# A hybrid attention layer: the mixing stage by a list schedule, its first merge moved forward, and two thresholds by bit search on ScalarE

## The chip, the core and the metric

The kernel runs on one core of a Trainium2 chip. The metric is the device time of one execution in microseconds (us); a time is the median of three runs. The engines are named as in the profile: PE multiplies matrices, PEld loads its weights, DVE is VectorE, ACT is ScalarE, POOL is GpSimd, SP issues DMAs. Each has its own queue of instructions.

## The reference, cut to what matters

One layer on 1024 tokens, ahead of which 16 meta tokens stand (1040 positions), with 1024 channels. Two half-step feed-forward parts (FFN1, FFN2; 2816 wide) stand around a mixing part:

```python
h = h + 0.5 * swiglu(rmsnorm(h, norm_ffn1[l]), ...)
u = rmsnorm(h, norm_mix[l])
qa, ka, va, qi, ki, wi, qs, ksw, vsw, ga, gb = jnp.split(u @ w_in[l], IN_SPLITS, axis=-1)
...                                     # rope on all queries and keys
o_sparse = sparse_branch(qa, ka, va, qi, ki, wi, pos, kvalid, topk)    # topk = 256
o_swa = swa_branch(qs, ksw, vsw, sinks[l], pos, kvalid)                # window 128, with sinks
merged = sigmoid(ga) * (o_sparse @ w_branch_sparse[l]) + sigmoid(gb) * (o_swa @ w_branch_swa[l])
h = h + merged @ w_out[l]
h = h + 0.5 * swiglu(rmsnorm(h, norm_ffn2[l]), ...)
```

The sparse branch works on blocks of 128 queries. An index score, the sum over 4 heads of relu(qi ki) wi, is computed for each query and key; each query keeps the 256 keys of the highest score (ties go to the lower position), and attention of 8 heads is taken over these.

## The kernel before

Positions lie along the free dimension, in two halves of 528 (with the meta tokens) and 512. Every f32 operand of a product is kept as a pair of f16 tiles, high and low part, and a product is three matmuls (`mm3`, L145 to L147). A weight is loaded by SP into `wst`; `split_w` (L130, L131) makes the pair `wsp`: ACT copies the high part, DVE computes the low one. `wsp` has four buffers, `wst` two.

The stages are FFN1, the mixing stage and FFN2. In the two FFN stages the kernel fixes the order of the engines' instructions by hand (`tc.manual_schedule(engines=ORDERED)`: PE, DVE, ACT, POOL). In the mixing stage it does not: the framework's scheduler orders what `layer_kernel` writes down, within the limits of the buffers. FFN1 ends with its down projection, the matmuls `pdn`; DVE adds each to `h`, and the squares of `h` are summed into `acc`. From that `norm_stats` makes `n_r` (a sum over the partitions on PE, `nsum`; small operations; a broadcast by PE, `nbc`) and `norm_u` the normed `un` and its pair `u`.

The mixing stage then consists of these pieces:

- `k_half`, `q_half`: projections (`rp`), rope (`rt` on DVE and POOL, `ry` on ACT) and a way through DRAM (`qscr`, `kscr`) that lays heads and rows out for the scores. `pv_t` is the value projection.
- `score(b)` for block b = 1 to 7 of the sparse branch: PE computes `ps_i`, ACT the ReLU `rel`, DVE sums into `sc`, 128 queries by 16 + 128 (b + 1) keys.
- `swa_block(b)`: scores `ps_s`, DVE adds mask and finds the maximum (`psw`), ACT exponentiates and sums (`a_sm`), PE transposes (`ptr`), ACT and DVE make the pair (`pts`), PE multiplies by the values, and the result is transposed into `oT` (`otr`).
- Thresholds. Block 0 needs none. Blocks 1 to 4 use `by_max`: rounds of MAX8 (the 8 largest of each row) and MATCH_REPLACE8 (strike them out), on DVE alone. Blocks 1 and 2 drop the lowest; block 3 (528 keys) and block 4 (656 keys) take 32 rounds each. Blocks 5 to 7 use `search((5, 6, 7))`: the 32 bits of each row's 256th largest score are found one after another. For each bit ACT runs a Sign pass over each block's scores with a sum (`jk`, L812), DVE compares the sum and makes the next candidate with operations of three columns (`s5d`, `s5key`, `s5nb`). `select(b, kth)` then turns scores into a mask (0 or a large negative number), ties included.
- `sparse_block(b)`: like `swa_block`, with `ps_a`, the mask added by DVE (`psp`, `b_mx`), `b_sm`, `ptb`.
- `swa_merge(d)` for 8 groups of channels: a gate (`p_gate`, tanh into `gt`), the branch's projection (`p_br`), their product `mg`. The same for the sparse branch, then the sum of both as a pair `mt`, and `p_out`, the projection back, added to `h`.

In `layer_kernel`'s text the first half's merge of the sparse branch (8 times 36 matmuls of 512 columns) and its projection (8 times 24) stand behind sparse block 7, in the same loop over the halves as the second half's.

Of the kernel before, what the change touches and what calls it, by code (L numbers as in the profile page):

```python
# [16 lines left out]
P = 128  # L17
# [14 lines left out]

WS = 256.0
# [6 lines left out]
F_GROUPS = ((0, 6), (6, 12), (12, 18), (18, 22))  # L40

# [14 lines left out]
def layer_kernel(ctx: ExitStack, tc: tile.TileContext, xT, gains, wgu1, wd1, win, wvi, wbs, wbw, wout,  # L56
                 wgu2, wd2, sinks, rope, m_swa0, m_swa, m_sp0, eye, out):
    nc = tc.nc
# [3 lines left out]
    ph = {}  # L62

# [22 lines left out]
    def mcst(shape, dt, name, bufs=1):
        return ph["sb"].tile(shape, dt, tag=name, name=name, bufs=bufs)

    def mmps(name):
        return ph["ps"].tile([P, 512], F32, tag="mm", name=name, bufs=3)  # L90

    def qkps(name):
        return ph["ps"].tile([P, 512], F32, tag="qk", name=name, bufs=2)

    def trps(name):
        if not ph["mix"]:
            return ph["ps"].tile([P, ph["S"], 512], F32, tag="w", name=name, bufs=8 // ph["S"])[:, 0, :]
# [19 lines left out]
    ident = cst.tile([P, P], F32, name="ident")  # L117
    nc.sync.dma_start(ident, eye)
    g_all = cst.tile([P, 4, KD], F32, name="g_all")
    nc.sync.dma_start(g_all, gains)  # L120
    ones = cst.tile([P, 1], F32, name="ones")
    nc.vector.memset(ones, 1.0)

    def load_raw(src, n):
        st = big.tile([P, 1024], F32, tag="wst", name="wst", bufs=2)
# [8 lines left out]
    def wsp_tile():  # L134
        return big.tile([P, 2, 1024], F16, tag="wsp", name="wsp", bufs=4)
# [27 lines left out]
    def new_acc():  # L163
        return big.tile([P, 528], F32, tag="acc", name="acc", bufs=2)
# [31 lines left out]
    def fpage(shape, dt, name):  # L196
        return ph["sb"].tile(shape, dt, tag="fp", name=name, bufs=27)

    def ftmp(name):
        return ph["sb"].tile([P, 528], F32, tag="ft", name=name, bufs=6)  # L200

    def fbtmp(name):
        return ph["sb"].tile([P, 528], F32, tag="fb", name=name, bufs=5)

    def wide(name):
        return ph["ps"].tile([P, ph["S"], 512], F32, tag="w", name=name, bufs=8 // ph["S"])
# [20 lines left out]
    def ffn(u, rb, hs, gi, wgu, wd, other_half, passes, saved):  # L227
# [10 lines left out]
        def new_hid(x):  # L238
# [6 lines left out]
            return big.tile(shape, F16, tag="nt", name="hid", bufs=2)  # L245
# [101 lines left out]
        def sum_tiles():  # L347
            return [ph["sb"].tile([P, 1024], F32, tag="wS", name=n_, bufs=2) for n_ in ("sa", "sb")]

        def late_tiles():  # L350
            return (ph["sb"].tile([P, 2, 1024], F16, tag="ws", name="x3", bufs=2),
                    ph["sb"].tile([P, 2, 512], F16, tag="w4", name="x4", bufs=2))
# [268 lines left out]
    hsp = dram.tile([KD, P, T], F32, name="hspill")  # L621
# [9 lines left out]
    open_phase("mix")  # L631

# [36 lines left out]
    def stack_q(ys, qt):  # L669
        scr = dram.tile([2, 2, P, 512], F16, tag="qscr", name="qscr", bufs=3)  # L670
# [6 lines left out]
    def stack_k(ys, kts, w):  # L677
        scr = dram.tile([2, P, 2, w], F16, tag=f"kscr{w}", name="kscr")
# [84 lines left out]
    def score(b):  # L763
        w = META + P * (b + 1)
        raw = ph["sb"].tile([P, w], F32, tag=f"sc{b}", name=f"sc{b}")
# [30 lines left out]
    def search(bs):  # L796
# [53 lines left out]
    def select(b, kth):  # L850
        w = META + P * (b + 1)
        raw = sc[b][0]
        gt = ph["sb"].tile([P, T], F16, tag="jk", name="gt", bufs=1)[:, :w]
        eq = ph["sb"].tile([P, T], F16, tag="eq", name="eq", bufs=1)[:, :w]
# [39 lines left out]
    def pttile(name):  # L894
        return ph["sb"].tile([P, 2, 1024], F16, tag="PT", name=name, bufs=2)

    def swa_block(b, qs, oT):
# [28 lines left out]
        pv = ph["ps"].tile([P, 512], F32, tag="pv", name="pv_s", bufs=1)  # L926
# [27 lines left out]
    def sparse_block(b, qa, oT):  # L954
# [6 lines left out]
        pv = ph["ps"].tile([P, 512], F32, tag="pv", name="pv_b", bufs=1)  # L961
# [25 lines left out]
    def new_oT():  # L987
        return ph["sb"].tile([P, 2, 4, 512], F16, tag="oT", name="oT", bufs=3)
# [14 lines left out]
    oT_w = []  # L1003
    for x in range(2):
# [16 lines left out]
    kth = search((5, 6, 7))  # L1021
    merged = [[], []]

    def swa_merge(d):
        gw, bw = load_w(win[12 + d], 1024), load_w(wbw[d], 512)
        for x in range(2):
            mg = hp([P, 512], F32, "mg")
# [4 lines left out]
    by_max(1)  # L1032
    by_max(2)
    sparse_block(0, qa, oT_s[0])
    sparse_block(1, qa, oT_s[0])
    sparse_block(2, qa, oT_s[0])
    swa_merge(0)
    swa_merge(1)
    swa_merge(2)
    by_max(3)  # L1040
    sparse_block(3, qa, oT_s[0])
    swa_merge(3)
    by_max(4)
# [158 lines left out]
```

## Time and profile before

| | us |
|---|---|
| median of 3 runs | 2033.18 (2031.63 to 2033.3) |
| profiled execution | 2033.16 |
| its span, first to last instruction | 2031.1 |
| PE busy | 1936.5 (95%) |
| DVE busy | 1627.2 (80%) |
| ACT busy | 901.0 (44%) |
| POOL busy | 386.9 (19%) |
| mixing stage, 682 to 1382: DVE busy | 574.8 |
| mixing stage, 682 to 1382: ACT busy | 422.4 |

Times in the trace count from the first instruction. The busy time of PE is that of matmuls that overlap, so it is no measure of how closely they follow each other. The mean clock granted to PE is 0.99 of full speed in the mixing stage.

### The profile page before, as it was taken

How to read it: one execution, taken by the hardware profiler on the slowest of the kernel's cores; microseconds unless marked ns; L12 is line 12 of the kernel's file. 1: busy time of each engine (PE TensorE's matmuls, PEld its weight loads, DVE VectorE, ACT ScalarE, POOL GpSimd, SP SyncE). 2: the span in 40 equal slices, each digit the busy share in tenths (PEclk: the TensorE clock that was granted, in tenths of full speed). 3: DMA queues.
4: the chain of work that ended last, by engine and by line, in shares of the span. 5: the costliest groups of instructions: out<-in, count | busy, mean ns of one | idle time of the engine just before them, and what ended most of it. 6: DMA issues, size and time to landing. Idle time of an engine off the chain costs nothing.

```text
span 2031.1 us, 32839 instructions
## 1 busy us (share of the span) xinstructions
PE 1936.5 (95%) x13080; PEld 1197.3 (59%) x13080; DVE 1627.2 (80%) x2779; ACT 901.0 (44%) x1602; POOL 386.9 (19%) x313
## 2 busy tenths in 40 slices
PE   5899999999999989899999999998899999999997
PEld 4588888888888556454545654444344444444443
DVE  7888788778875799999999964566987787788767
ACT  4433233333323446589885643433433243233232
POOL 3611312221310132221001000002322212312200
PEclk9999999999999999999999999999999999999998
DMA  4011111111113543212020024241112121111213
GB/s 158 11 63 48 58 63 50 55 64 58 48 63 105 183 141 112 99 59 73 17 63 17 27 68 156 78 164 49 34 55 68 48 72 47 63 62 47 76 38 130
DMA packets 58873, 146.95 MB, mean 72 GB/s; under 512 B 7264, under 2 KB 13408, under 8 KB 58720
## 3 DMA queue, kind: packets, MB, share of 16 engines
q1 hardware_dynamic: 58720, 144.86, 22.3%
q8 instruction: 102, 1.67, 0.3%
q14 instruction: 51, 0.42, 0.1%
HBM read 130.01 MB, written 14.76 MB: 71 GB/s over the span
## 4 chain that ended last, share of the span: by engine, by line
PE 70%; DVE 18%; ACT 4%; issue 4%; DMA 2%; POOL 2%; DVEq 0%; SPq 0%; ACTq 0%; POOLq 0%
PE pc L327 14%; PE pd L327 14%; PE pa L327 14%; PE pb L327 7%; PE p_br L999 2%; DVE sc L791 2%; DVE u L222 2%; DVE wsp L131 1%; PE p_gate L147 1%; PE p_gate L145 1%; PE p_gate L146 1%; DVE m L790 1%; PE p_out L146 1%; PE p_out L147 1%; PE p_out L145 1%
## 5 line engine op out<-in xcount | busy, mean ns | idle before, releaser
L327 PEld LDWEIGHTS <-wsp 128*128 128x128 f16 x4176 | 410.0, 98 | 214.2 <-issue 12.3
L327 PEld LDWEIGHTS <-x 128*128 128x128 f16 x3132 | 307.3, 98 | 157.9 <-issue 8.5
L327 PE MATMUL pa<-u,wsp 128*128 128x264 f16 (+1 forms) x1440 | 224.7, 310 | 0.0
L131 DVE SCALAR_TENSOR_TENSOR wsp<-wst,wsp 128x1024 f16<-128x1024 f32 (+2 forms) x130 | 134.8, 1038 | 54.6 <-ACT wsp L130 54.3
L130 ACT ACTIVATE wsp<-wst 128x1024 f16<-128x1024 f32 (+2 forms) x130 | 111.7, 863 | 140.1 <-PE p_out L147 45.9
L147 PEld LDWEIGHTS <-wsp 128*128 128x128 f16 x912 | 90.5, 99 | 94.5 <-issue 12.3
L145 PEld LDWEIGHTS <-wsp 128*128 128x128 f16 x912 | 91.0, 100 | 85.1 <-issue 4.1
L146 PEld LDWEIGHTS <-wsp 128*128 128x128 f16 x912 | 90.7, 99 | 80.2 <-issue 3.9
L327 PE MATMUL pb<-tb,wsp 128*128 128x264 f16 (+1 forms) x720 | 113.7, 312 | 8.1 <-ACT tb L235 5.5
L327 PE MATMUL pc<-tb,x 128*128 128x264 f16 (+1 forms) x720 | 113.9, 313 | 6.6 <-DVE c L458 6.4
L327 PE MATMUL pc<-tb,wsp 128*128 128x256 f16 (+1 forms) x720 | 114.2, 314 | 0.0
L327 PE MATMUL pd<-tb,x 128*128 128x256 f16 (+1 forms) x720 | 110.7, 308 | 0.0
L327 PE MATMUL pd<-u,x 128*128 128x256 f16 (+1 forms) x720 | 110.7, 308 | 0.0
L289 POOL TENSOR_TENSOR t<-g,g 128x512 f32<-128x512 f32 x16 | 25.5, 1595 | 436.0 <-DVE g L494 436.0
L812 ACT ACTIVATE jk<-sc,s5nb 128x784 f16<-128x784 f32 (+2 forms) x93 | 97.9, 1052 | 19.0 <-DVE s5nb L827 15.3
L341 ACT ACTIVATE wsp<-sa 128x1024 f16<-128x1024 f32 (+1 forms) x62 | 60.2, 971 | 103.4 <-DVE sa L393 103.4
L327 PE MATMUL pa<-hid,wsp 128*128 128x264 f16 (+1 forms) x648 | 103.1, 310 | 0.0
L341 ACT ACTIVATE wsp<-wst 128x1024 f16<-128x1024 f32 (+1 forms) x62 | 59.9, 967 | 94.3 <-DMA wst<-in_wgu_dram 49.9
L327 PE MATMUL pd<-hid,x 128*128 128x256 f16 (+1 forms) x648 | 101.6, 308 | 0.0
L147 PE MATMUL p_gate<-u,wsp 128*128 128x512 f16 x256 | 97.0, 379 | 1.4 <-DVE wsp L131 1.4
L145 PE MATMUL p_gate<-u,wsp 128*128 128x512 f16 x256 | 97.0, 379 | 0.0
L146 PE MATMUL p_gate<-u,wsp 128*128 128x512 f16 x256 | 97.0, 379 | 0.0
(234 smaller groups left out, 4147.6 us busy)
## 6 DMA issues: line engine op xcount, KB each, us to landing
wst<-in_wgu_dram SPq DMA_DIRECT2D x88, 512.0 KB, 3.7
wst<-in_win_dram SPq DMA_DIRECT2D x44, 512.0 KB, 3.5
wst<-in_wd_dram SPq DMA_DIRECT2D x48, 384.0 KB, 3.4
wst<-in_wd_dram SPq DMA_DIRECT2D x32, 256.0 KB, 2.7
wst<-in_wout_dram SPq DMA_DIRECT2D x16, 512.0 KB, 4.1
qscr<-ry SPq DMA_DIRECT2D x20, 256.0 KB, 2.1
q<-qscr SPq DMA_DIRECT2D x20, 256.0 KB, 3.0
wst<-in_wbs_dram SPq DMA_DIRECT2D x16, 256.0 KB, 2.7
```

Of the source, the lines that this page charges most:

```text
L130: nc.scalar.activation(sp[:, 0, :n], st[:, :n], AF.Copy, scale=WS)
L131: nc.vector.scalar_tensor_tensor(sp[:, 1, :n], st[:, :n], WS, sp[:, 0, :n], op0=ALU.mult, op1=ALU.subtract)
L145: nc.tensor.matmul(ps, w[:, 0, wcols], xt[:, 0, xcols], start=start, stop=False)
L146: nc.tensor.matmul(ps, w[:, 0, wcols], xt[:, 1, xcols], start=False, stop=False)
L147: nc.tensor.matmul(ps, w[:, 1, wcols], xt[:, 0, xcols], start=False, stop=stop)
L222: nc.vector.tensor_sub(u[k][:, 1, s0:s1], t[:, :w], u[k][:, 0, s0:s1])
L289: nc.gpsimd.tensor_sub(vb(t1), vb(b1), va(a1)[:, :, :wb])
L327: nc.tensor.matmul(ps[:, s, :n], w[:, a, wc], tiles[k][:, y, s * stride:s * stride + n], start=start and k == 0 and j == 0, stop=stop and ...
L341: nc.scalar.activation(sp[:, 0, :n], st[:, :n], AF.Copy, scale=WS)
L791: nc.vector.match_replace(out=raw, in_to_replace=m8, in_values=raw, imm_value=MARK)
L812: nc.scalar.activation(junk[:, :w], sc[b][0], AF.Sign, bias=bias[:, j:j + 1], accum_out=s[:, j:j + 1])
L999: nc.tensor.matmul(pb, bw[:, a, c * P:(c + 1) * P], oT[:, y, c, :], start=c == 0 and n == 0, stop=c == 3 and n == 2)
```

## The change

Only the mixing stage is changed. Three things are done.

First, the stage's operations are no longer issued as they are written down. A class `Plan` stands in place of `nc`: between `nc.start()` and `nc.run()` it records each operation with an estimated cost and the operations that it depends on. `run` then makes a list schedule: it steps through simulated clocks of the five queues, always takes the operation that can start first, of several the one written first, grants pool buffers in the order written, and at the end issues everything in that order under `tc.manual_schedule(engines=ORDERED)`. Its clocks all begin at nothing, whatever FFN1 has left over.

Second, the text of the stage is reordered: the first half's merge and its projection stand among the sparse blocks 4 to 7, some `swa_merge` stand elsewhere.

Third, blocks 3 and 4 find their threshold by `search((3,))` and `search((4,))`, each right behind its `score`, and get a `select`; `by_max` remains for blocks 1 and 2. A search over one block has the same 32 passes, small operations of one column. `gt` in `select` has a tag of its own; the scratch `jk` has one buffer for all three searches.

In the changed kernel every recorded operation has the line of a helper (L312 for the planned ones, L185 for those issued directly), so names of tiles, not lines, tell what a row is. Tiles of the searches are called `s3...`, `s4...` and `s5...`.

The core of the diff:

```diff
+    def cost(eng, op, outs, ins):
...
+            if isinstance(rhs, View) and rhs.dt == F16:
+                return max(n, 64) / 2400 + 0.004, n / 2400 + 0.17
...
+        if eng == "ACT":
+            return 0.055 + n * 0.00088, 0.15 + n * 0.00088
...
+        t = 0.077 + n * k * 0.00104 + (0.06 if op == "match_replace" else 0)
+        return t, t + 0.083
...
+        if engine.name == "ACT" and "accum_out" in kw:
+            busy, done = busy + 0.1, done + 0.19
...
+        clock = dict.fromkeys(names, 0.0)
...
+        while len(order) < count:
...
+            t, e = best
+            i = heapq.heappop(now[e])[1] if now[e] else heapq.heappop(future[e])[2]
+            clock[e] = t + busy
...
+        with self.tc.manual_schedule(engines=ORDERED):
+            for i in order:
...
-    nc = tc.nc
+    nc = Plan(tc.nc, tc)
...
     open_phase("mix")
+    nc.start()
...
-        gt = ph["sb"].tile([P, T], F16, tag="jk", name="gt", bufs=1)[:, :w]
+        gt = new(ph["sb"], [P, T], F16, tag="gt", name="gt", bufs=1)[:, :w]
...
             if b:
                 score(b)
+                if b in (3, 4):
+                    kth.update(search((b,)))
...
-    kth = search((5, 6, 7))
+    kth.update(search((5, 6, 7)))
...
-    by_max(3)
-    sparse_block(3, qa, oT_s[0])
...
+    select(3, kth[3])
+    sparse_block(3, qa, oT_s[0])
+    swa_merge(3)
+    swa_merge(4)
+    select(4, kth[4])
+    swa_merge(5)
+    oT_s.append(new_oT())
+    swa_merge(6)
+    sparse_block(4, qa, oT_s[1])
+    swa_merge(7)
+    select(5, kth[5])
+    for d in range(2):
+        sparse_merge(0, d, mT0)
+    sparse_block(5, qa, oT_s[1])
+    for d in range(2, 6):
+        sparse_merge(0, d, mT0)
+    select(6, kth[6])
+    sparse_block(6, qa, oT_s[1])
+    for d in range(6, 8):
+        sparse_merge(0, d, mT0)
+    project_out(0, 0, 4, mT0, acc)
+    select(7, kth[7])
+    sparse_block(7, qa, oT_s[1])
+    project_out(0, 4, 8, mT0, acc)
+    mT1 = []
+    for d in range(KD):
+        sparse_merge(1, d, mT1)
+        if d == 3:
+            ffn2_norm(0, acc)
...
+    project_out(1, 0, 8, mT1, acc)
+    nc.run(h2[0] + h2[1] + u3[0] + rb3 + [acc])
```

Three places show what this does to the engines' orders. The first is the stage's start on DVE. The `h` is the last one of FFN1's down projection; the `wsp` behind it are the first two weights of `k`. Before:

```order
L588 SCALAR_TENSOR_TENSOR h<-pdn,h 128x512
L222 TENSOR_TENSOR u<-un,u 128x256
L131 SCALAR_TENSOR_TENSOR wsp<-wst,wsp 128x1024
L222 TENSOR_TENSOR u<-un,u 128x256
L219 SCALAR_TENSOR_TENSOR un<-h,g_all,nbc 128x256
L131 SCALAR_TENSOR_TENSOR wsp<-wst,wsp 128x1024
L222 TENSOR_TENSOR u<-un,u 128x256
```

After, from the middle of the second half's statistics (`n_e` and `n_r` are their last small operations); between that `h` and these rows stand five adds of squares:

```order
L312 TENSOR_TENSOR n_e<-n_r 128x4
L312 TENSOR_TENSOR n_e<-n_e,n_a 128x4
L312 TENSOR_SCALAR n_e<-n_e 128x4
L312 TENSOR_TENSOR n_r<-n_r,n_e 128x4
L312 SCALAR_TENSOR_TENSOR un<-h,g_all,nbc 128x512 x2
L312 TENSOR_TENSOR u<-un,u 128x512 x2
L312 SCALAR_TENSOR_TENSOR un<-h,g_all,nbc 128x512 x2
L312 TENSOR_SCALAR snk_7754<-snk 128x8
L312 TENSOR_TENSOR u<-un,u 128x512 x2
L312 SCALAR_TENSOR_TENSOR un<-h,g_all,nbc 128x512 x2
L312 SCALAR_TENSOR_TENSOR wsp<-wst,wsp 128x1024
```

The statistics of the second half and six `un` of 512 columns with four `u` now stand between that `h` and the first split weight of `k`; before, one half-width `u` did.

The second place is ACT, where block 3's scores end. `rel` is the ReLU of index scores, `ry` a rope result. Before:

```order
L773 ACTIVATE rel<-ps_i 128x272 x4
L773 ACTIVATE rel<-ps_i 128x400 x3
L130 ACTIVATE wsp<-wst 128x1024
L773 ACTIVATE rel<-ps_i 128x400
L773 ACTIVATE rel<-ps_i 128x272
L665 ACTIVATE ry<-rt_8321 128x512
L130 ACTIVATE wsp<-wst 128x1024
L773 ACTIVATE rel<-ps_i 128x272 x3
L773 ACTIVATE rel<-ps_i 128x256
```

After:

```order
L312 ACTIVATE jk,s3S<-sc_8324,s3z 128x528
L312 ACTIVATE wsp<-wst 128x1024
L312 ACTIVATE jk,s3S<-sc_8324,s3nb 128x528
L312 ACTIVATE wsp<-wst 128x1024
L312 ACTIVATE jk,s3S<-sc_8324,s3nb 128x528
L312 ACTIVATE ry<-rt_8422 128x512
L312 ACTIVATE ry<-rt_8490 128x512
L312 ACTIVATE jk,s3S<-sc_8324,s3nb 128x528
L312 ACTIVATE wsp<-wst 128x980
```

A Sign pass of block 3's search stands between every one or two other operations, where rope results, weight splits and later blocks' scores followed one another.

The third place is DVE around the merge of the first half: `oT` is the end of a sparse block, `gt`, `mg` and `mt` belong to the merge. Before, at the last block:

```order
L1072 SCALAR_TENSOR_TENSOR mt<-gt,mt 128x512
L884 TENSOR_TENSOR o<-pv_b,b_rec 128x512
L892 TENSOR_TENSOR oT<-otr,oT 128x4x128
L131 SCALAR_TENSOR_TENSOR wsp<-wst,wsp 128x1024
L1069 SCALAR_TENSOR_TENSOR gt<-gt,p_br 128x512
L131 SCALAR_TENSOR_TENSOR wsp<-wst,wsp 128x512
L1070 TENSOR_TENSOR gt<-gt,mg 128x512
L1072 SCALAR_TENSOR_TENSOR mt<-gt,mt 128x512
L131 SCALAR_TENSOR_TENSOR wsp<-wst,wsp 128x1024
L1069 SCALAR_TENSOR_TENSOR gt<-gt,p_br 128x512
```

After, at the end of block 4:

```order
L312 SCALAR_TENSOR_TENSOR gt<-gt,p_br 128x512
L312 TENSOR_TENSOR oT<-otr,oT 128x4x128
L312 TENSOR_TENSOR gt<-gt,mg 128x512
L312 SCALAR_TENSOR_TENSOR wsp<-wst,wsp 128x512
L312 TENSOR_TENSOR s5d<-s5S,s5thr 128x3
L312 SCALAR_TENSOR_TENSOR s5key<-s5d,s5key 128x3
L312 TENSOR_TENSOR s5val<-s5key,s5flip 128x3
L312 SCALAR_TENSOR_TENSOR mt<-gt,mt 128x512
L312 TENSOR_SCALAR jk,s5cnt<-sc_9813,s5val 128x784
L312 TENSOR_SCALAR jk,s5cnt<-sc_9951,s5val 128x912
```

The first half's merge now begins around the end of block 4 and the last bit of the search for blocks 5 to 7, and alternates with block 5's threshold; before, six of its eight groups came behind block 7.

## Rows read from the trace of the kernel before

**Rows 1.** Timeline of PE at the stage's two ends: start, duration, line, operation, names.

```profile
681.90 0.38 PE L147 MATMUL pdn<-hid,wsp 128*128 128x512 f16 x1
...
1381.94 0.38 PE L147 MATMUL p_out<-mt,wsp 128*128 128x512 f16 x1
```

**Rows 2.** Chain that ended last, 1180 to 1200: start us, us, what.

```profile
1179.91 0.77 PE ptr L872 x7
...
1191.82 2.59 PE p_br L999 x12
```

**Rows 3.** Windows: length, busy PE PEld DVE ACT POOL, clock, DMA share, GB/s.

```profile
682.00:1190.00 508.00, 477.17 (x3823) 280.18 (x3822) 472.83 (x1260) 350.64 (x780) 83.95 (x118) 0.99 0.22 72
1190.00:1384.00 194.00, 191.40 (x894) 87.48 (x893) 103.47 (x139) 73.33 (x101) 0.00 (x0) 1.00 0.38 124
859.10:1068.60 209.50, 199.94 (x1463) 107.91 (x1461) 203.20 (x607) 180.39 (x417) 26.34 (x50) 1.00 0.17 54
682.00:781.00 99.00, 87.58 (x572) 54.15 (x571) 82.84 (x191) 46.42 (x98) 26.03 (x24) 0.95 0.43 137
```

**Rows 4.** Waits of PE, 682 to 1190: total us, times, longest us.

```profile
PE ps_s L756 <- DMA q<-qscr: 6.2, 3, 2.8
PE ps_i L756 <- ACT rel L773: 5.3, 7, 1.5
...
PE rp L145 <- DVE un L219: 3.5, 1, 3.5
```

**Rows 5.** Groups of DVE by form, 682 to 1384: busy us, mean ns, idle before.

```profile
L131 DVE SCALAR_TENSOR_TENSOR wsp<-wst,wsp 128x1024 f16<-128x1024 f32 x64 | 82.2, 1284 | 47.5 <-ACT wsp L130 47.2
L790 DVE MAX8 m<-sc 128x8 f32<-128x656 f32 x32 | 26.8, 838 | 0.2
L791 DVE MATCH_REPLACE8 sc<-m,sc 128x656 f32<-128x656 f32 x32 | 26.5, 827 | 0.0
L790 DVE MAX8 m<-sc 128x8 f32<-128x528 f32 x32 | 22.4, 701 | 0.0
L791 DVE MATCH_REPLACE8 sc<-m,sc 128x528 f32<-128x528 f32 x32 | 22.2, 693 | 0.0
...
L161 DVE TENSOR_TENSOR acc<-acc,sq 128x512 f32<-128x512 f32 x19 | 13.1, 687 | 0.3
L219 DVE SCALAR_TENSOR_TENSOR un<-h,g_all,nbc 128x512 f32<-128x512 f32 x16 | 11.3, 744 | 2.4 <-PE nbc L191 2.4
L222 DVE TENSOR_TENSOR u<-un,u 128x512 f16<-128x512 f32 x16 | 10.6, 690 | 2.2 <-ACT u L221 2.1
...
L815 DVE TENSOR_TENSOR s5d<-s5S,s5thr 128x3 int32<-128x3 f32 x32 | 5.6, 175 | 1.8 <-ACT jk L812 1.6
...
L829 DVE SCALAR_TENSOR_TENSOR s5key<-s5d,s5key 128x3 int32<-128x3 int32 x31 | 4.8, 156 | 0.1
```

**Rows 6.** Groups of ACT by form, 682 to 1384, same columns.

```profile
L812 ACT ACTIVATE jk<-sc,s5nb 128x784 f16<-128x784 f32 x31 | 29.4, 947 | 18.4 <-DVE s5nb L827 15.3 <-DVE b_ng L973 3.0
...
L812 ACT ACTIVATION_READ_ACCUMULATOR jk<-sc,s5nb 128x1 f32 x93 | 18.0, 193 | 0.0
...
L974 ACT ACTIVATE psp<-psp,b_ng 128x656 f32<-128x656 f32 x8 | 6.7, 842 | 0.0
...
L974 ACT ACTIVATE psp<-psp,b_ng 128x528 f32<-128x528 f32 x8 | 5.8, 730 | 0.0
```

**Rows 7.** Timeline of DVE from the last Sign pass to block 5's mask.

```profile
1072.80 0.16 DVE L815 TENSOR_TENSOR s5d<-s5S,s5thr 128x3 int32<-128x3 f32 x1 [0.79 <-ACT jk L812]
...
1091.27 0.57 DVE L864 TENSOR_SCALAR sc<-eq 128x784 f32<-128x784 f16 x1
```

**Rows 8.** Timeline of PE and DVE behind the last `pdn`.

```profile
685.78 0.39 PE L145 MATMUL rp<-u,wsp 128*128 128x272 f16 x1 [3.50 <-DVE un L219]
...
682.75 0.69 DVE L588 SCALAR_TENSOR_TENSOR h<-pdn,h 128x512 f32<-128x512 f32 x1
...
683.68 1.23 DVE L131 SCALAR_TENSOR_TENSOR wsp<-wst,wsp 128x1024 f16<-128x1024 f32 x1
```

More of the change, by code (lines that the diff above doesn't have):

```diff
@@ new lines, with __init__, real, overlap @@
+class Lazy(View):
+    def __init__(self, shape, dt, make, key, bufs, whole):
+        View.__init__(self, self, (), shape, dt)
+        self.make, self.key, self.bufs, self.whole = make, key, bufs, whole
+        self.made = None
+        self.live = False
+        self.seen = []
+        self.last = self.first = None
+    def real(self):
+        if self.made is None:
+            self.made = self.make()
+        return self.made
+def overlap(a, b):
+    return a is None or b is None or all(x0 < y1 and y0 < x1 for (x0, x1), (y0, y1) in zip(a, b))
@@ L62, in layer_kernel, with new @@
     ph = {}
+    def new(pool, shape, dt, tag=None, name=None, bufs=1):
+        return nc.tile(pool, shape, dt, tag or name, name, bufs, pool is ph.get("ps"))
     def open_phase(name):
@@ L134, in wsp_tile @@
     def wsp_tile():
-        return big.tile([P, 2, 1024], F16, tag="wsp", name="wsp", bufs=4)
+        return new(big, [P, 2, 1024], F16, tag="wsp", name="wsp", bufs=4)
     def load_w(src, n, st=None):
@@ L163, in new_acc @@
     def new_acc():
-        return big.tile([P, 528], F32, tag="acc", name="acc", bufs=2)
+        return new(big, [P, 528], F32, tag="acc", name="acc", bufs=2)
     def norm_stats(acc, subs):
@@ L244, in new_hid @@
                 return hp(shape, F16, "hid")
-            return big.tile(shape, F16, tag="nt", name="hid", bufs=2)
+            return new(big, shape, F16, tag="nt", name="hid", bufs=2)
         made = [0]
@@ L620, in layer_kernel @@
     u2 = []
-    hsp = dram.tile([KD, P, T], F32, name="hspill")
+    hsp = new(dram, [KD, P, T], F32, name="hspill")
     def mix_norm(x, r):
@@ L677, in stack_k @@
     def stack_k(ys, kts, w):
-        scr = dram.tile([2, P, 2, w], F16, tag=f"kscr{w}", name="kscr")
+        scr = new(dram, [2, P, 2, w], F16, tag=f"kscr{w}", name="kscr")
         for half in range(2):
@@ L894, in pttile @@
     def pttile(name):
-        return ph["sb"].tile([P, 2, 1024], F16, tag="PT", name=name, bufs=2)
+        return new(ph["sb"], [P, 2, 1024], F16, tag="PT", name=name, bufs=2)
     def swa_block(b, qs, oT):
@@ L987, in new_oT @@
     def new_oT():
[L988 removed]
+        return new(ph["sb"], [P, 2, 4, 512], F16, tag="oT", name="oT", bufs=3)
     def gated(x, gw, bw, oT):
@@ L1079, in layer_kernel, with project_out @@
+    def project_out(x, d0, d1, mT, acc):
         c0 = META if x == 0 else HS0[1]
-        for d in range(KD):
+        for d in range(d0, d1):
             w = load_w(wout[d], 1024)
```

343 lines of the change are left out of this document (270 added, 73 removed).

## The prediction

> **What bounds the kernel now.** I read the page first, then the windows of the mixing stage, PE's waits there, the groups by form on DVE and ACT, and the timeline at the stage's two ends. The other two stages keep their instructions and their order, so only the mixing stage can move: from the last `pdn` matmul of FFN1, which ends at 682.3, to the last `p_out` at 1382.3 [rows 1], 700 us of the span of 2031.1.
>
> PE is the engine to count there, but its busy time hides the room in it. In a queue that never waits, `p_br` matmuls of 512 columns follow each other every 2.59 / 12 = 0.216 us [rows 2], while one of them is shown as busy for 0.38 us [rows 1]. So I walked down the order of both kernels and added 0.216 us for each 512 columns (in proportion for narrower ones) and, for each transposition, 0.77 / 7 = 0.11 [rows 2]. That gives 627 us for the stage, the same in both kernels, since none of PE's instructions is added or removed; 73 us of the 700 are therefore PE's waits. They are unevenly spread. The windows show 682 to 1190 (the stretch that ends with the last sparse block) and 1190 to 1384 (the second half's merge and projection) [rows 3]: the first holds 437 us of counted work in 508, the second, to 1382.3, 190 in 192. By busy time the first would hide only 508 - 477 = 31 us. The Trainium skill (Perfetto Trace Analysis, section Identifying the Most-Contended Engine) says the same of matmul busy time in general, that it is a poor measure of headroom because matmuls are pipelined; with it as the measure no more than 31 us could be won before 1190, with the count 71.
>
> Within that stretch DVE is the engine that is full. From 859.1 to 1068.6, the 31 bits of the search for blocks 5 to 7, it is busy 203.2 of 209.5 us, ACT 180.4 [rows 3]. PE's waits name many releasers and none is large: queries from the scratch buffer 6.2 us, `rel` 5.3, `un` for the first `rp` 3.5 [rows 4].
>
> **The change part by part.**
>
> *Thresholds of blocks 3 and 4.* DVE loses 32 MAX8 and 32 MATCH_REPLACE8 of each width: 26.8 + 26.5 + 22.4 + 22.2 = 97.9 us [rows 5], and 88 once the overlapped tail of each of them (0.08 us) is taken off. It gains two searches of 31 bits with about three small operations a bit. At three columns one takes 0.156 to 0.175 us [rows 5]; at one column no row shows it, so between 0.07 (0.156 without the tail) and 0.175: 13 to 33 us. Two more `select` and two counts are some 10 us. DVE is lighter by 45 to 65 us, all of it in the stretch where it is full. ACT gains 32 Sign passes of 528 and 32 of 656 columns. Exponentials of these widths take 730 and 842 ns and each Sign pass has a read of its sum, 193 ns, behind it [rows 6]: 62 us, 50 without the tails; I take 58; that these passes cost nothing or less is excluded, since ACT does not have them before.
>
> *What that makes the critical resource.* The scratch tile `jk` has one buffer, given out in program order, so the searches of block 3, of block 4 and of blocks 5 to 7 run one after another on ACT. Going down ACT's order in the same way, with the mean of each form less a tail of 0.10 us, ACT has 41 us of work ahead of the first Sign pass and 341 us from the first to the last; in between stand the rope copies, probabilities and weight splits. Three terms follow.
>
> First Sign pass: in 682 to 781 ACT does 55 us of counted work in 99, at which pace 41 us take 74; from PE's side it is 48 us of counted work to block 3's last scores, 15.5 idle (below) and some 5 for the sums, 69. I take 74.
>
> The 341 us: ACT's share of time decides. Before, in the search, it is 180.4 / 209.5 = 86%, and 18.4 of the 29.1 idle us stand before a Sign pass, released by DVE's `s5nb` for 15.3 [rows 6], which sits behind MAX8 and MATCH_REPLACE8. Those, of blocks 3 and 4, are gone. Without the 18.4 the share is (180.4 + 18.4) / 209.5 = 95%. That gives 341 / 0.95 = 359 us. The bounds are 341 (never idle) and 341 / 0.86 = 396.
>
> From the last Sign pass to block 5's mask: before from 1072.8 to 1091.8, 19 us [rows 7]; DVE's order has the same chain after it, with about as much other work in between. So block 5 may begin at 74 + 359 + 19 = 452 us after the start.
>
> *First half's merge among the sparse blocks.* The order shows PE with 395 us of counted work up to the point where block 5's scores need the mask, and 232 behind it. To this come the 2 that the second half's end loses now and 8 for the waits of blocks 5 to 7 (before, their stretch holds 83 us of counted work; at the mean rate of waits, 71 / 437 = 16%, it would lose 13, at the rate of the end 1): 242. PE alone would reach that point at 395 + 15.5 + waits; with before's rate of waits outside the start, (71 - 3.5) / 437 = 15%, this is 471; with a third of them gone, for a DVE that is no longer full, 451. The two ways meet at about 450; ACT's 452 is what I use. The last part, the second half's merge and projection, keeps its order.
>
> *The start.* Before, PE is idle for 3.50 us between the last `pdn` and the first `rp`; DVE splits the first weights of `k` at 683.68, right behind the last `h` [rows 8]. After, the plan starts all its clocks at nothing and DVE's queue holds, behind that `h`: five adds of squares at 0.61 us (687 ns less the tail), the statistics (eight small operations through DVE, ACT and PE; some 2 us, an estimate), then six `un` of 0.66 and four `u` of 0.61 [rows 5], and only then the first `wsp`, 1.2. That is 683.4 + 3.0 + 2 + 4 + 2.4 + 1.2 = 696 us, and with a wait between them 697.8 for `rp`, so PE is idle for 15.5 us instead of 3.5: 12 more. Later DVE does not have to do those, so part comes back; it costs the most where PE's count is the bound, and nothing if ACT's chain is. In 682 to 781 the granted clock is 0.95 [rows 3], that is about 10 us at 1.2 GHz after such a wait. The Trainium skill (TensorE: Matmul & The Clock Gate, Part 1) states that the throttled clock is the default and activity releases it; by that rule the longer wait would add another 2 to 3 us, which I leave out of the sum. The trace agrees as far as that 0.95 goes.
>
> **The sum.** 452 + 242 = 694 us against 700: -6, on the profiled execution's 2033.2 (2031.1 of span and 2.1 around it), which is the median of the three runs: 2027.
>
> **The rivals.** (1) *Packs tighter.* ACT is never idle between the Sign passes, because PE and DVE are ahead of it: 74 + 341 + 19 + 242 = 676, -24, so 2009. For it: DVE is lighter by some 50 us and waits in the order stand far from their releasers. Against: PE's waits outside the start must fall from 68 to 434 - 395 - 15.5 = 23 us. (2) *Three searches in series hold back block 5.* On the other side: each bit is a round trip from ACT to DVE and back, now 95 of them in one chain instead of 31, and DVE's queue is strictly in order, with weight splits of 1284 ns [rows 5] in front of the small operations. If ACT keeps only before's share of 86%: 74 + 396 + 19 + 242 = 731, +31, so 2064; half way, at 90%, 2048. It decides from a share of 93% downwards, where the sum is 700. For it: even before, with a third as many round trips, ACT's idle time stood mostly there. (3) *Nothing moves*, since PE's waits are only relocated: 2033; the start's 12 us and less DVE work would cancel.
>
> **How the numbers follow.** The forecast, ACT at 93 to 97%, is 2018 to 2034 and has 0.38; rival 1, 2005 to 2018, 0.24; rival 2, 2039 to 2064, 0.28; rival 3, 2030 to 2038, 0.10. A measurement of this kernel tells 0.2%, 4 us, from no change, so the borders are 2029 and 2037. Below lie rival 1 and two thirds of the forecast, 0.24 + 0.25, between them a third of the forecast and most of rival 3, 0.20, above rival 2 and the rest, 0.31. With one tenth left out at each end the range is 2006 to 2056; the likeliest case's own is 2018 to 2034.
>
> **What would show it.** PE idle for about 15 us from 682, and the granted clock below 0.95 in the first 100 us. The first Sign pass of block 3 at about 756 and the last of blocks 5 to 7 at about 1115, that is 2.8 us for a bit of one block and 5.5 for one of three; ACT idle before Sign passes for less than 20 us in all. DVE busy some 50 us less over the stage. From block 5's mask to the last `p_out` some 240 us. I would be wrong if bits of one block take over 3 us, if PE waits long for ACT or DVE outside the search, or if the last 240 us lose more than 10.

## The result: slower by 0.8%, and the profile after

| | us |
|---|---|
| before, median in the same job | 2032.55 (2031.63 to 2033.3) |
| after, median of 4 runs | 2050.85 (2047.44 to 2052.19) |
| ratio after / before | 1.0083, 95% interval 1.0071 to 1.0096 |
| span of the profiled execution, before / after | 2031.1 / 2050.2 |

The prediction was 2027, a gain of 6 us; measured is a loss of 18. The time lies inside the range of 2006 to 2056, but on the wrong side of no change.

The windows of the changed kernel (length, busy PE, PEld, DVE, ACT and POOL, granted clock, DMA share, GB/s), to be read against [rows 3]:

```profile
682.00:781.00 99.00, 78.61 (x472) 47.27 (x473) 69.14 (x144) 39.80 (x72) 24.43 (x21) 0.88 0.38 125
781.00:881.00 100.00, 81.12 (x628) 51.79 (x627) 90.34 (x287) 69.94 (x183) 23.17 (x17) 0.90 0.32 103
881.00:981.00 100.00, 90.55 (x719) 53.00 (x717) 88.65 (x323) 81.89 (x226) 22.27 (x27) 1.00 0.19 63
981.00:1402.00 421.00, 417.44 (x2906) 225.70 (x2905) 282.99 (x687) 282.10 (x530) 13.12 (x53) 1.00 0.24 76
```

Everything is lost in the first 300 us (682 to 981): PE is busy for 79 to 91 of 100 us there, at a granted clock of 0.88 and 0.90 in the first two hundred, and in the remaining 421 us it hardly waits at all. The kernel before, over the same 299 us and in the second of the three windows:

```profile
682.00:981.00 299.00, 275.18 (x2073) 162.58 (x2072) 278.81 (x736) 204.12 (x490) 71.02 (x78) 0.98 0.30 98
781.00:881.00 100.00, 91.34 (x759) 56.16 (x757) 97.10 (x244) 67.91 (x170) 25.43 (x18) 1.00 0.29 94
```

PE is idle for 48.7 of the 299 us after and for 23.8 before. Block 5, whose mask comes only after the last Sign pass at 1143.5, holds nobody back.

PE's timeline behind the last `pdn` answers to [rows 1, 8]:

```profile
683.73 3.91 PE L185 MATMUL pdn<-hid,wsp 128*128 128x512 f16 x10 [2.51 <-DVE wsp L185]
692.30 1.84 PE L312 MATMUL nsum<-ones,acc 128*128 128x1 f32 x8 [4.66 <-DVE acc L185]
695.63 2.08 PE L312 MATMUL nbc<-ident,n_r 128*128 128x128 f32 x8 [1.50 <-DVE n_r L312]
703.52 1.06 PE L312 MATMUL rp<-u,wsp 128*128 128x272 f16 x4 [5.81 <-ACT wsp L312]
705.76 6.47 PE L312 MATMUL rp<-u,wsp 128*128 128x272 f16 x33 [1.17 <-DVE wsp L312]
```

The statistics and the norm stand in front of the first `rp`, as the order said: 703.52 instead of 685.78. Of these 17.7 us, 12.4 are the longer way from the last `pdn` (it ends at 687.64) to `rp`: 15.9 instead of 3.5. Of the 15.9 PE is idle for 12.0; the rest are the matmuls of the statistics, `nsum` and `nbc`. The other 5.3 lie ahead of it: a `pdn` waits 2.51 us for its weight split, because FFN1's last split moved behind two more `h` on DVE. Behind that wait the granted clock was 0.59 from 683.70 to 687.70 in this execution, and the ten `pdn` took 3.91 us; in the profiled execution of plan_bymax, a run below with the same wait, they took 2.33. That is another 1.6:

```profile
682.60 2.33 PE L185 MATMUL pdn<-hid,wsp 128*128 128x512 f16 x10 [2.51 <-DVE wsp L185]
```

The last us is no more than the spread of the last `pdn` between runs: with FFN1 in its old order it ends at 681.96 in hold20_bymax and at 683.28 in hold20.

For the rest I count much as in the prediction (the stage's work comes to 630 us here, 3 more than there): the time since the last `pdn`, less the counted work that PE has done by then, is what PE has lost.

| PE's work done, us | 30 | 120 | 240 | all |
|---|---|---|---|---|
| before | 9.1 | 24.2 | 44.8 | 69.8 |
| after | 21.9 | 51.0 | 73.3 | 83.3 |

Up to 30 us of work 12.8 are lost at the start; to 240 another 15.7; behind that the changed kernel loses 10.0 where the kernel before loses 25.0, a gain of 15. Of the 28.5 us lost more up to 240, some 24 are idle time of PE. The few that are left fit the low clock, which by the mean clocks of the windows lasted some 40 us instead of some 10. In the stretch that loses, DVE's groups of the two new searches, 768 to 985 (busy us, mean ns, idle before):

```profile
L312 DVE SCALAR_TENSOR_TENSOR s4key<-s4d,s4key 128x1 int32<-128x1 int32 x31 | 8.9, 286 | 0.3
L312 DVE SCALAR_TENSOR_TENSOR s3nb<-s3key,s3flip 128x1 int32<-128x1 int32 x31 | 8.0, 257 | 0.0
L312 DVE SCALAR_TENSOR_TENSOR s3key<-s3d,s3key 128x1 int32<-128x1 int32 x31 | 7.8, 252 | 0.0
L312 DVE TENSOR_TENSOR s3d<-s3S,s3thr 128x1 int32<-128x1 f32 x32 | 7.7, 242 | 1.2 <-ACT jk L312 1.2
L312 DVE TENSOR_TENSOR s4d<-s4S,s4thr 128x1 int32<-128x1 f32 x32 | 7.6, 236 | 5.8 <-ACT jk L312 5.8
L312 DVE SCALAR_TENSOR_TENSOR s4nb<-s4key,s4flip 128x1 int32<-128x1 int32 x31 | 7.0, 226 | 0.2
```

One column takes longer than three columns did in [rows 5], 47.0 us for 188 operations. Where it goes can be seen at 788 to 795 (timeline of POOL, DVE and PE; lines between them are left out):

```profile
787.66 3.09 POOL L312 TENSOR_TENSOR rt<-rt,rt 128x512 f32<-128x512 f32 x2 [7.87 <-DVE s3key L312]
790.71 2.27 POOL L312 TENSOR_TENSOR ry<-rt,ry 128x512 f16<-128x512 f32 x2
```

```profile
788.17 0.77 DVE L312 SCALAR_TENSOR_TENSOR s3nb<-s3key,s3flip 128x1 int32<-128x1 int32 x1
...
790.09 0.67 DVE L312 TENSOR_TENSOR s3d<-s3S,s3thr 128x1 int32<-128x1 f32 x1
...
791.18 0.70 DVE L312 SCALAR_TENSOR_TENSOR s3key<-s3d,s3key 128x1 int32<-128x1 int32 x1
...
792.35 0.64 DVE L312 SCALAR_TENSOR_TENSOR s3nb<-s3key,s3flip 128x1 int32<-128x1 int32 x1
...
794.51 0.14 DVE L312 TENSOR_TENSOR s3d<-s3S,s3thr 128x1 int32<-128x1 f32 x1
```

```profile
786.26 0.81 PE L312 MATMUL rp<-u,wsp 128*128 128x512 f16 x3
794.10 1.01 PE L312 MATMUL ps_s<-k,q 128*128 128x256 f16 x4 [7.02 <-DVE a_mx L312]
```

While POOL works on the rope, an operation of one column takes 0.64 to 0.77 us, and behind POOL again 0.14. The ends tell what it waits for: `s3d` ends at 790.76 and POOL's `rt` at 790.75, the second `s3nb` at 792.99 and POOL's `ry` at 792.98. So it is with every held-up operation of the two searches: it lasts until the POOL operation beside it is done. The mask and maximum of the SWA scores stand behind them in DVE's queue, and PE waits for these 7.02 us. Of that the four held-up operations account for 2.2 (2.8 instead of 0.6); the rest is other work in the same queue at its usual pace, above all the rope, MAX8 and MATCH_REPLACE8 of block 2 and a weight split. Behind this wait PE's granted clock was 0.50 from 789.40 to 799.60. The Trainium skill (SBUF — State Buffer, section Who interferes with whom) states that a DVE instruction with two SBUF inputs contends with a GpSimd instruction that reads SBUF, and that one with at most one, outside DVE's two-port modes, does not. The trace agrees with the first half; on the second the run hold20_oneinput below was made, and its means, 0.141 to 0.148 us, agree.

The kernel before has the same hold-up, in weight splits, which read two SBUF operands too (DVE, then POOL):

```profile
744.12 2.29 DVE L131 SCALAR_TENSOR_TENSOR wsp<-wst,wsp 128x1024 f16<-128x1024 f32 x1
```

```profile
743.87 1.46 POOL L664 TENSOR_TENSOR rt<-rt,rt 128x512 f32<-128x512 f32 x1 [2.05 <-DVE rt L663]
```

Four of its 64 splits of 1024 columns took 2.1 to 2.3 us, each begun while POOL ran `rt`; the others took 1.2.

### The profile page after: what moved, and what is told of

The parts are those of the page before. It is cut to its first block, busy times and chain, and to the rows that moved or that the text cites. A ratio compares the mean times of both kernels' runs of the same rounds, so it can differ in the third digit from the quotient of the medians.

```text
span 2050.2 us, 33074 instructions
## 1 busy us (share of the span) xinstructions
PE 1935.7 (94%) x13080; PEld 1207.2 (59%) x13080; DVE 1581.3 (77%) x2819; ACT 950.9 (46%) x1730; POOL 385.9 (19%) x313
## 4 chain that ended last, share of the span: by engine, by line
PE 75%; DVE 14%; ACT 6%; issue 2%; POOL 1%; DMA 1%; SPq 0%; DVEq 0%; ACTq 0%; POOLq 0%
PE pc L185 15%; PE pd L185 14%; PE pa L185 14%; PE pb L185 7%; PE p_gate L312 6%; PE p_out L312 4%; PE pdn L185 4%; PE p_br L312 3%; ACT jk L312 3%; DVE sc L312 2%; DVE u L185 1%; PE ptr L312 1%; PE rp L312 1%; PE pv_b L312 1%; DVE tb L185 1%
## 5 line engine op out<-in xcount | busy, mean ns | idle before, releaser
L185 PEld LDWEIGHTS <-wsp 128*128 128x128 f16 x5136 | 507.2, 99 | 311.6 <-issue 34.4
L185 PEld LDWEIGHTS <-x 128*128 128x128 f16 x3132 | 307.3, 98 | 157.2 <-issue 7.9
L312 PEld LDWEIGHTS <-wsp 128*128 128x128 f16 x2160 | 208.1, 99 | 208.6 <-ACT wsp L312 6.1
L185 PE MATMUL pa<-u,wsp 128*128 128x264 f16 (+1 forms) x1440 | 224.7, 310 | 0.0
L312 PE MATMUL p_gate<-u,wsp 128*128 128x512 f16 x768 | 185.5, 379 | 0.0
L185 POOL TENSOR_TENSOR h<-h,base 128x512 f32<-128x512 f32 (+1 forms) x72 | 116.3, 1616 | 291.1 <-DVE base L185 229.7
L185 ACT ACTIVATE wsp<-wst 128x1024 f16<-128x1024 f32 (+2 forms) x104 | 90.4, 870 | 165.0 <-DMA wst<-in_wd_dram 56.3
L312 PE MATMUL rp<-u,wsp 128*128 128x512 f16 (+2 forms) x624 | 146.3, 374 | 9.0 <-ACT wsp L312 5.8
L312 DVE SCALAR_TENSOR_TENSOR wsp<-wst,wsp 128x1024 f16<-128x1024 f32 (+1 forms) x88 | 95.6, 1088 | 34.3 <-ACT wsp L312 33.3
L185 PE MATMUL pb<-tb,wsp 128*128 128x264 f16 (+1 forms) x720 | 114.0, 312 | 7.9 <-ACT tb L185 5.6
L185 PE MATMUL pc<-tb,x 128*128 128x264 f16 (+1 forms) x720 | 113.8, 313 | 5.6 <-DVE c L185 5.5
L185 PE MATMUL pc<-tb,wsp 128*128 128x256 f16 (+1 forms) x720 | 115.1, 316 | 0.0
L185 PE MATMUL pd<-u,x 128*128 128x256 f16 (+1 forms) x720 | 111.0, 308 | 0.0
L185 PE MATMUL pd<-tb,x 128*128 128x256 f16 (+1 forms) x720 | 110.7, 308 | 0.0
L185 ACT ACTIVATE wsp<-sa 128x1024 f16<-128x1024 f32 (+1 forms) x64 | 62.3, 973 | 103.3 <-DVE sa L185 103.2
L185 DVE SCALAR_TENSOR_TENSOR wsp<-wst,wsp 128x1024 f16<-128x1024 f32 (+2 forms) x104 | 104.8, 1007 | 5.9 <-ACT wsp L185 5.8
L185 POOL TENSOR_TENSOR t<-g,g 128x512 f32<-128x512 f32 x16 | 25.5, 1594 | 436.0 <-DVE g L185 436.0
L312 ACT ACTIVATE wsp<-wst 128x1024 f16<-128x1024 f32 (+1 forms) x88 | 81.2, 926 | 54.7 <-PE p_out L312 21.7
L185 PE MATMUL pa<-hid,wsp 128*128 128x264 f16 (+1 forms) x648 | 103.1, 310 | 0.0
L185 PE MATMUL pd<-hid,x 128*128 128x256 f16 (+1 forms) x648 | 101.6, 308 | 0.0
L312 ACT ACTIVATE jk<-sc,s5nb 128x784 f16<-128x784 f32 (+2 forms) x93 | 97.9, 1053 | 7.4 <-DVE s5nb L312 5.2
L185 ACT ACTIVATE base<-pa 128x528 f32<-128x528 f32 (+1 forms) x64 | 38.3, 598 | 132.3 <-PE pa L185 132.3
```

The costliest lines, as they stand in the source:

```text
L185: return getattr(engine.real, op)(*[give(a) for a in args], **{k: give(v) for k, v in kw.items()})
L312: getattr(engine.real, op)(*[give(a) for a in args], **{k: give(v) for k, v in kw.items()})
```

## The experiments

Three theories at first: A, the start costs everything; B, the two searches cost, where they run; C, the list schedule's order is worse than the framework's as such. The ratios are those to the kernel before, in the same job.

**hold20.** The plan may start the operations of the second half's norm only at 20 us of its clock (`ready` begins with the hold instead of 0):

```diff
-        ready = [0.0] * count
+        ready = list(self.holds)
...
+            nc.hold = 20.0
             mix_norm(1, norm_stats(acc, SUB_ALL[1]))
+            nc.hold = 0.0
```

> The changed kernel, but the list schedule may start the second half's statistics and norm (nsum, n_a to n_r, un, u) only 20 us after its zero; nothing is left out. In the order this puts the first two splits of k's weights ahead of them on DVE again, and with them FFN1's last weight split goes back to its old place. Theory A (the start costs everything: 4.4 us at FFN1's last pdn, 12.4 us of idle PE and some 2 of the low clock; the rest of the stage cancels out): 2032 to 2036. Theory B (the searches of blocks 3 and 4 slow the first 120 us of PE's work by their operations on DVE and ACT): the start's loss reappears there, 2040 to 2047. Theory C (the list schedule's order is worse than the framework's everywhere): 2043 to 2050.

2036.55 (2033.04 to 2039.0), ratio 1.0008 (0.9999 to 1.0018): 14.3 less than the changed kernel, just above A's 2032 to 2036. The last `pdn` has no wait for its weights any more, and the first `rp` starts at 685.42, as before:

```profile
680.74 2.54 PE L187 MATMUL pdn<-hid,wsp 128*128 128x512 f16 x11
685.42 0.61 PE L315 MATMUL rp<-u,wsp 128*128 128x272 f16 x4 [2.15 <-DVE un L187]
689.26 3.13 PE L315 MATMUL rp<-u,wsp 128*128 128x272 f16 x13 [3.23 <-DVE wsp L315]
```

**plan_bymax**: the two lines `kth.update(search((b,)))` and the selects of blocks 3 and 4 out, `by_max(3)` and `by_max(4)` in.

> The changed kernel with by_max for blocks 3 and 4 again (MAX8 and MATCH_REPLACE8 on DVE, no search, no select for them); list schedule and the moved merge stay. Theory A: the start stays as it is, DVE is full again among the sparse blocks: 2048 to 2060. Theory B: 2030 to 2040. Theory C: 2055 to 2070.

2037.4 (2033.19 to 2042.33), ratio 1.0020 (1.0010 to 1.0030), 13.5 less than the changed kernel, with its bad start unchanged. B is right too: the searches cost, although they relieve DVE, and A, by which the start costs everything, is not.

**before_search**, the opposite: the kernel before, `by_max(3)` and `by_max(4)` replaced by searches and selects.

> The kernel before, only with search and select for blocks 3 and 4 in place of by_max, each search right behind its scores; no list schedule, merge at its old place. Theory A: the start is that of before, DVE is lighter by some 50 us where it is full: 2015 to 2030. Theory B: the searches cost 10 us or more, 2040 to 2055. Theory C: 2015 to 2025.

2079.16, ratio 1.0222 (1.0207 to 1.0237). Without the list schedule the same searches cost 45 us. Of the three only B had the sign, and its range ended at 2055; A and C had expected a gain. The six groups of small operations take 46.9 us here, as in the changed kernel (47.0), so the threefold cost does not lie in them.

**noplan**: the changed kernel without `nc.start()` and `nc.run()`, the framework orders the stage.

> The changed kernel's text without the list schedule: every operation of the mixing stage is issued as written and the framework's scheduler orders it; searches and moved merge stay. Theory A: the start is that of before, 2015 to 2035. Theory B: 2040 to 2060. Theory C: 2010 to 2025, clearly faster than the kernel before.

2072.5, ratio 1.0190 (1.0175 to 1.0206), 22 more than with the list schedule and above every range. With the searches in it, C falls. Against before_search, which has the searches but the old order of the text, it is 6.7 less: so much the reordered text is worth without the list schedule.

**hold20_bymax**: both corrections together.

> The list schedule and the moved merge with both corrections: norm of the second half not before 20 us of the schedule's clock, and by_max for blocks 3 and 4 as in the kernel before (no search for them); nothing is left out. Theory A+B (start and searches are two separate losses of about 15 and 13 us, the rest of the schedule is a gain): 2019 to 2026, faster than the kernel before. Rival (DVE, full again, eats up what the start gives back): 2031 to 2037.

2021.78, ratio 0.9936 (0.9923 to 0.9948). Faster than the kernel before; the two losses add (with `by_max` the start is worth 15.6, with the searches 14.3).

**hold20_bymax_oldmerge**: in its text, all `sparse_merge(0, d, mT0)` and `project_out(0, ...)` behind `sparse_block(7, ...)`.

> hold20_bymax with the first half's merge and projection written behind sparse block 7 again, the other moves of the text kept. If the moved merge is what fills PE's waits among the sparse blocks: 10 to 20 us slower than hold20_bymax. If the list schedule fills them by itself (it can take later operations as soon as their buffers are granted): within 3 us of it.

2035.74, ratio 1.0012 (1.0003 to 1.0022), 14 more than hold20_bymax. With the merge at its old place PE has nothing to fill in among the last sparse blocks; the window of 1081 to 1181, first without the move, then (hold20_bymax) with it:

```profile
1081.00:1181.00 100.00, 90.95 (x912) 58.80 (x912) 92.06 (x248) 64.30 (x132) 9.83 (x23) 0.98 0.08 25
```

```profile
1081.00:1181.00 100.00, 99.59 (x819) 58.23 (x816) 89.64 (x214) 62.61 (x124) 5.70 (x19) 1.00 0.21 67
```

So each part of the change has its price, each step against the one above it (the first step holds the other moves of the text as well):

| kernel | us | step |
|---|---|---|
| before | 2033.6 | |
| list schedule, other moves of the text, start mended (hold20_bymax_oldmerge) | 2035.7 | +2 |
| and first half's merge moved (hold20_bymax) | 2021.8 | -14 |
| and searches for blocks 3 and 4 (hold20) | 2036.6 | +15 |
| and the start as it was planned (after) | 2050.9 | +14 |

Open was why a search costs 15 us. B1: its small operations are held up while GpSimd runs. B2: its round trips between ACT and DVE cost, GpSimd or not. **hold20_dverope** and **hold20_bymax_dverope** put the rope's two GpSimd operations on DVE:

```diff
-                nc.gpsimd.tensor_tensor(out=t1[:, :w], in0=t1[:, :w], in1=t2[:, :w], op=op)
+                nc.vector.tensor_tensor(out=t1[:, :w], in0=t1[:, :w], in1=t2[:, :w], op=op)
...
-                nc.gpsimd.tensor_sub(y[:, 1, c0 - o:c1 - o], t1[:, :w], y[:, 0, c0 - o:c1 - o])
+                nc.vector.tensor_sub(y[:, 1, c0 - o:c1 - o], t1[:, :w], y[:, 0, c0 - o:c1 - o])
```

> hold20 (search for blocks 3 and 4, start mended) with the two GpSimd operations of each rope group on VectorE, so that nothing of the search meets GpSimd at work. Some 20 us in which small operations of the search were held up go, some 27 us of rope work (44 operations of 0.61 us) come to VectorE. It is read only against hold20_bymax_dverope. Theory B1 (the search costs because its small operations are held up while GpSimd works): no more than 5 us slower than hold20_bymax_dverope. Theory B2 (the search costs by its round trips in the strict orders of ScalarE and VectorE, with or without GpSimd): 10 to 16 us slower than that.

> hold20_bymax with the rope's GpSimd operations on VectorE; the other half of the pair. VectorE gets 27 us more work in the part where it is full with MAX8: both theories 2025 to 2045; what tells them apart is the difference to hold20_dverope.

2011.86, ratio 0.9892 (0.9877 to 0.9907), and 2023.25, ratio 0.9948 (0.9934 to 0.9962). The search is now 11 us faster than `by_max`, whose 2023 lies below the range given for it. This speaks for B1, but the pair is not clean: with `by_max` DVE has no room for the rope, and PE stands at one place for 18.8 us. Its longest wait, 682 to 1426 (total us, times, longest us):

```profile
PE ps_a L315 <- DVE b_mx L315: 19.9, 3, 18.8
```

At 240 us of PE's work, ahead of that place, search and `by_max` have lost 61.5 and 50.4 with the rope on GpSimd, 31.4 and 26.5 with it on DVE: the difference falls from 11 to 5, and both lose 24 to 30 less. So the rope on GpSimd costs either kind, as the held-up weight splits of the kernel before suggest.

**hold20_oneinput** asks the question directly: the order of hold20 in every row, and only the three small operations of a bit changed, in the searches of one block. The plan still records the operation with two operands, and so makes the same order; what is issued in its place is set by `nc.swap`. The masks of blocks 3 and 4 become others by it, but no operation's place or size depends on them:

```diff
+                if i in self.swaps:
+                    op, args, kw = self.swaps[i]
...
+            if n == 1:
+                nc.swap = ("tensor_scalar", (d, s, float(2 * TOPK - 1 - META - P * (bs[0] + 1)), None),
+                           {"op0": ALU.is_ge})
             nc.vector.tensor_tensor(out=d, in0=s, in1=thr, op=ALU.is_ge)
...
+            if n == 1:
+                nc.swap = ("tensor_scalar", (nb, key, 1 << k, -2 ** 31),
+                           {"op0": ALU.bitwise_or, "op1": ALU.bitwise_xor})
             nc.vector.scalar_tensor_tensor(nb, key, 1 << k, flip, op0=ALU.bitwise_or, op1=ALU.bitwise_xor)
...
+            if n == 1:
+                nc.swap = ("tensor_scalar", (key, d, k, 2 ** 30),
+                           {"op0": ALU.logical_shift_left, "op1": ALU.bitwise_or})
             nc.vector.scalar_tensor_tensor(key, d, k, key, op0=ALU.logical_shift_left, op1=ALU.bitwise_or)
```

> hold20 in exactly its order, but the three small VectorE operations of each bit of the searches of blocks 3 and 4 read one SBUF operand instead of two: the comparison takes its threshold as a constant, the candidate and the key are made with constants, so these two thresholds are not those of the reference (the key does not collect its bits). In hold20 these operations take 240 to 286 ns in the mean where 145 is their usual time, some 20 us in all, nearly all of it while GpSimd runs. Theory B1 (that hold-up is what the searches cost): the mean falls to about 150 ns and the time to 2021 to 2028, near hold20_bymax. Theory B2 (round trips in the strict orders): 2033 to 2037, as hold20, even if the means fall. From the pair with the rope on VectorE about half of it, 2028 to 2032, is my own expectation.

2017.58 (2016.96 to 2020.43), ratio 0.9924 (0.9911 to 0.9936): 19 less than hold20, more than B1 had asked for and more than the half that I expected. (The 240 to 286 ns named ahead of the run are not hold20's; its six groups have means of 204 to 350.) It is also 4 less than hold20_bymax, but there the intervals overlap. DVE's groups, 750 to 970, in hold20 and then here:

```profile
L315 DVE SCALAR_TENSOR_TENSOR s3nb<-s3key,s3flip 128x1 int32<-128x1 int32 x31 | 10.8, 350 | 0.0
L315 DVE TENSOR_TENSOR s4d<-s4S,s4thr 128x1 int32<-128x1 f32 x32 | 8.9, 279 | 10.4 <-ACT jk L315 10.3
```

```profile
L322 DVE TENSOR_SCALAR s3nb<-s3key 128x1 int32<-128x1 int32 x31 | 4.4, 141 | 0.0
L322 DVE TENSOR_SCALAR s4d<-s4S 128x1 int32<-128x1 f32 x32 | 4.7, 148 | 10.5 <-ACT jk L322 10.4
```

All six groups together take 48.1 us in hold20 and 27.5 here: 20.6 us of DVE's time for 19 us of the kernel's. One small operation still reads two operands here, at the end of block 3's search, and it is as slow as ever; in hold20 it took 1252 ns, here 1246:

```profile
858.87 1.25 DVE L322 SCALAR_TENSOR_TENSOR s3key<-s3car,s3low 128x1 uint16<-128x1 f32 x1
```

The way to PE can be read too, in its waits for the maximum of the SWA scores (682 to 1000) and in the windows, first hold20 and then hold20_oneinput:

```profile
PE ps_s L315 <- DVE a_mx L315: 9.2, 8, 3.7
682.00:981.00 299.00, 260.54 (x1914) 155.28 (x1913) 262.82 (x794) 202.66 (x512) 74.27 (x70) 0.97 0.31 99
```

```profile
PE ps_s L322 <- DVE a_mx L322: 2.5, 4, 1.6
682.00:981.00 299.00, 271.44 (x2050) 162.54 (x2047) 256.56 (x833) 219.53 (x554) 76.47 (x77) 0.99 0.30 99
```

PE is idle for 10.9 us less there, and its mean clock is 0.99 instead of 0.97; so the 19 us are not DVE's 20.6 passed on one for one. The read of a second SBUF operand while GpSimd reads is what made the searches dear; the round trips, which are the same here, cost no more than the relief of DVE gives back. The lost time at 240 us of PE's work falls from 61.5 to 43.7, below the 44.8 of the kernel before.

**hold20_dverope_s4**: hold20_dverope with `by_max(3)` and the search for block 4 alone.

> hold20_dverope with by_max for block 3 and the search for block 4 alone. VectorE gets some 35 us of MAX8 and MATCH_REPLACE8 back, ScalarE loses 27 us of Sign passes and one search leaves the series. If VectorE's work is the limit once the rope lies on it (hold20_bymax_dverope stood 18.8 us at one place): 2014 to 2022. If the series of searches is: 2003 to 2010.

2014.52, ratio 0.9902 (0.9887 to 0.9917): at the lower end of the range for DVE's work as the limit. It is 2.7 slower than with both searches, but the intervals overlap, so which of the two is better stays open.

**before_dverope**: the kernel before with the rope on DVE.

> The kernel before with the rope's GpSimd operations on VectorE, nothing else. If GpSimd's slowness at the rope is a cost of its own that the kernel before has too: 2015 to 2030. If VectorE, which is full from 781 to 1081, has no room for the 27 us: 2035 to 2055.

2057.18, ratio 1.0117 (1.0103 to 1.0131), 2 above the range for a DVE without room; PE waits 23.1 us at one place for `b_mx`. The lowest median of all has hold20_dverope: it is the changed kernel with the start mended and the rope on DVE, and DVE has the room for it because of the searches.

## Why the prediction was wrong

*The chain of terms.* First Sign pass, predicted 74 us after the last `pdn` of before: it started at 768.05, 85.8 after 682.3, of which 5.3 are the late `pdn`. From the first to the last Sign pass 359 were predicted; from 768.05 to 1144.7 it is 377, an ACT share of 341 / 377 = 90% instead of 95%. From there to the last `p_out` (1401.2) 261 were predicted and 256.5 measured. These add up to 719, but as the second route showed, PE's own, it is not this chain that PE stood at: from 981 on PE waits for 4 us of 421. What is true of it is that the same held-up operations made the passes late and PE late: in hold20_oneinput the chain from first to last pass and the stage as a whole are both 18 us shorter than in hold20. A sign of being wrong that was named came true for block 3: by the first and last `s3nb`, `s4nb` and `s5nb` a bit took 3.5 us there, 2.9 in block 4 and 5.2 in the three blocks together.

*The step that failed* is the price of a small operation of one column, "between 0.07 and 0.175": it measured 0.226 to 0.286 in the mean, 47.0 us in place of 13 to 33, and up to 1.2 us for one. In the sum it stands behind the 95% of ACT's share and behind the third of PE's waits that was to go: the first took it that small operations are late only when MAX8 stands in front of them, the second that a DVE with less to do holds PE up less. I took the price from rows in a stretch where POOL was mostly idle and carried it into one where POOL runs for 22 to 24 us of each hundred. A row of the kernel before would have warned, the view of the tile `s5nb` (shortest, median and longest duration in ns, first and last start):

```profile
L827 DVE SCALAR_TENSOR_TENSOR s5nb<-s5key,s5flip x31: 120/154/1069, 859.1 to 1068.6; 128x3 int32<-128x3 int32 x31
```

Its longest is seven times its median. I put the late `s5nb` down to MAX8 in front of them, which holds up an operation's start but not its duration.

*The start* was sized rightly where it was seen: 15.9 us from the last `pdn` to `rp` for 15.5 predicted. That is luck in part: the statistics and their broadcast took 5.6 us instead of 2 (692.15 to the first `un` at 697.75), while `rp`, at 703.52, waited only for ACT's half of the weight and started ahead of DVE's split (704.48), for which, with a wait behind it, the sum had 3. And I took FFN1 to keep its order, but its last weight split moved on DVE, which cost 2.5 us at once and with the low clock behind it 4.1 of the 5.3. That the start's loss would partly come back was wrong: 14 us came back only when it was mended. By the granted clock, 0.88 and 0.90 in the first two windows where the kernel before has 0.95 and 1.00, the sentence on the clock was right in direction, and the low clock came again at later stops of PE (0.50 from 789.40 to 799.60).

*A third of PE's waits gone because DVE is lighter*: the waits outside the start up to 240 us of work grew. The gain came behind that, and hold20_bymax shows what it comes from: with `by_max` and DVE at 93 of 100 us busy PE loses just as little there:

```profile
981.00:1081.00 100.00, 100.00 (x623) 51.47 (x622) 93.00 (x249) 81.11 (x157) 2.14 (x11) 1.00 0.16 48
```

The moved merge gives the 14 us, under the list schedule; the prediction gave it no term of its own. That PE is filled with other work, not that DVE is relieved, takes its waits away there.

*The rivals.* Rival 2 gave the right sign for half a reason: the searches do cost, by 15 us with the schedule and 45 without it, but not by holding back block 5. Rival 1's tight packing is what PE does from 981 on.

*Open*: why the framework's order makes the searches three times as dear as the list schedule (the small operations take as long in both), and what the moved merge alone would give without the list schedule and without the searches, which was not run.

## What to carry to other kernels

Price a small operation in the stretch into which it moves, with the engines that run beside it, and look at the maximum beside the median: a group whose mean is far above its median is held up by something, and in this kernel a tiny two-operand operation on DVE paid with the rest of the GpSimd operation that it met. A planned order whose clocks all begin at nothing takes what is ready at nothing first; look at its first rows for work that stands in front of what PE needs next. To fill PE's waits, dense work that is free to move was worth more here (14 us) than relief for the engine that seemed full.

## What was not expected of the hardware

A DVE operation on 128 x 1 elements with two SBUF operands that began while POOL ran a 128 x 512 TENSOR_TENSOR took 0.52 to 1.22 us in the changed kernel, up to the end of that POOL operation, and 0.15 otherwise; beside POOL's MEMSET, which only writes, two of them took 0.16. With one operand they took 0.141 to 0.148 in the mean, in the same places of the same order. MAX8 kept its 0.57 us for 400 columns beside POOL, and the rope's first products, which read one operand in PSUM and one in SBUF (`rt` from `rp`, 128 x 512), their 0.68.
